# Spreading the choice of experts over 18 pairs of weight tiles, with GpSimd splitting the weights of the first 8

## The chip, the cores and the metric

The kernel runs on one core of one Trainium2 chip. The metric is device time in microseconds (us) of one execution; three timed runs of the kernel before gave 1732.83, 1733.56 and 1734.88 us, a median of 1733.56 us.

## The reference

Two transformer blocks over 256 tokens and 16 meta tokens, width 1024, all in float32. The change lies in the last layer, a mixture of 16384 small experts:

```python
def peer_layer(h, w_q, sub_keys, u_tab, v_tab):
    q = (hf @ w_q).reshape(T, PEER_HEADS, 2, PEER_DQ // 2)
    s = jnp.einsum('thpd,hpnd->thpn', q, sub_keys)
    sc, idx = lax.top_k(s, PEER_TOPK)                    # 16 of 128 keys, per head and half
    cand = (sc[:, :, 0, :, None] + sc[:, :, 1, None, :])  # 256 pairs
    top_sc, pos = lax.top_k(cand, PEER_TOPK)             # 16 of 256 pairs
    eidx = jnp.take_along_axis(cidx, pos, axis=-1)
    gate = jax.nn.softmax(top_sc)
    act = gelu(u_tab[eb] . hb)                           # per token, its 128 experts
    y = sum(gate * act * v_tab[eb])
```

There are 8 heads, 128 keys in each half, 256 tokens. What comes before (a first block with attention and two feed-forward parts, then a gated recurrence and a convolution) is not touched.

## The kernel before, in words

The kernel does not gather experts. It computes the activation of all 16384 experts for all 256 tokens, and multiplies by a gate that is zero for those not chosen. The table `peer_u` is 128 tiles of 128 x 1024 float32 (512 KB each). Matrix products are made exact enough by splitting every float32 operand into a high and a low part: `weights_by_part` (lines 89 to 101) loads a tile `wraw` by DMA, casts it to `whi` on ScalarE (ACT, L99), and subtracts, `wlo = wraw - whi` (L100), on VectorE (DVE) or, where the caller says so, on GpSimd (POOL). `mm3` (lines 116 to 119) then makes three matmuls of each 128 x 128 block on TensorE (PE): L117 and L118 with `whi`, L119 with `wlo`. A tile is 8 blocks, 24 matmuls. In the experts `wraw`, `whi` and `wlo` have three buffers each, so a tile's cast waits until PE is done with the tile three before it.

The loop over `m` goes over 64 pairs of tiles: `expert_acts(m, e)` makes the 48 matmuls of a pair, with `e` as the engine of the split, and a Gelu (ACT, L1351) takes the result to `acts`.

Beside it DVE chooses the experts. The generator `choosing` does this in steps, each ending at a `yield`: `keys_of(q)` for the last two heads (the others are done earlier, beside the query matmuls); `pairs(i)` for each half i of the tokens, which adds the two key scores to 256 candidates (L1234), casts indices (L1236), finds the best 16 for two heads in each step (`sixteen`, L1218 to L1222), and takes the found positions apart by two integer operations and a cast (L1241 to L1243); `members(i)`, which looks the indices up by a comparison (L1248), a product (L1250) and a sum (L1252). The loop over `m` advances the generator by two steps for each pair as long as `m < DIRECT`. From pair DIRECT on the softmax is made and `gates` builds the gate matrices, 64 of them, 1.5 for each pair.

The first `yield` in `keys_of` has no value, so `next(steps, 0)` gives None at the first step, and `alone` turns False in pair 0: the splits of all 64 pairs are on DVE in the program as built, and the trace shows none of `peer_u` on POOL.

A scheduler puts each engine's instructions into one fixed list; an engine runs its list in order, and waits at an instruction until its operands and buffers are there.

Of the kernel before, what the change touches and what calls it, by code (L numbers as in the profile page):

```python
# [46 lines left out]
def two_blocks(ctx: ExitStack, tc: tile.TileContext, A, out):  # L47
    nc = tc.nc
    act, vec, pool, pe = nc.scalar, nc.vector, nc.gpsimd, nc.tensor
# [34 lines left out]
    def bank(name):  # L84
        ids = banks[-1][name]
        ids.append(ids.pop(0))
        return ps.tile([128, 512], F32, name=name, tag=f"bank{ids[-1]}")
# [28 lines left out]
    def mm3(o, wh, wl, xh, xl, first, last):  # L116
        pe.matmul(o, lhsT=wh, rhs=xh, start=first, stop=False)  # L117
        pe.matmul(o, lhsT=wh, rhs=xl, start=False, stop=False)  # L118
        pe.matmul(o, lhsT=wl, rhs=xh, start=False, stop=last)  # L119
# [62 lines left out]
    with psum(mm=8):  # L182
        o = bank("mm")
# [925 lines left out]
    def experts(hx):  # L1109
        NEGL = -3.0e38  # L1110

        GATE = 2.0 ** 14
        DIRECT = 17
        PACE = 1.5
        es = ExitStack()
        early = ExitStack()
# [2 lines left out]
        def wt(ap, e=None, parts=1):  # L1119
            return weights(ap, e=e, parts=parts, four=False)  # L1120
# [8 lines left out]
        for i in range(2):  # L1129
            for e2 in range(2):  # L1130
                o = bank("sc")
# [10 lines left out]
        for n in range(6):  # L1142
            o = bank("mm")
            project(o[:, :S + 2], wt(A["peer_wq"][n], vec if n == 1 else pool), raw, t1=S + 2)
            rp.append(o)
            if n == 0:
                o = bank("sc")
# [76 lines left out]
        def keys_of(q):  # L1224
            for i in range(2):
                for e2 in range(2):
                    sixteen(best[i][:, q, e2], idx[i][:, q, e2], score(q, i)[:, e2])
            yield
# [3 lines left out]
        def pairs(i):  # L1232

            vec.tensor_tensor(out=cand[i], in0=best[i][:, :, 0][:, :, :, None].to_broadcast(wide),  # L1234
                              in1=best[i][:, :, 1][:, :, None, :].to_broadcast(wide), op=ALU.add)
            vec.tensor_copy(idf[i], idx[i])  # L1236
            for q in range(NH):
                sixteen(st[i][2][:, q], pos[i][:, q], cand[i][:, q].rearrange("p a b -> p (a b)"))
                if q % 2:
                    yield  # L1240
            vec.tensor_scalar(ab[i][:, 0], pos[i], 4, None, op0=ALU.logical_shift_right)  # L1241
            vec.tensor_scalar(ab[i][:, 1], pos[i], 15, None, op0=ALU.bitwise_and)
            vec.tensor_copy(abf[i], ab[i])  # L1243

        def members(i):

            for e2 in range(2):
                vec.tensor_tensor(out=cand[i], in0=abf[i][:, e2][:, :, :, None].to_broadcast(wide),  # L1248
                                  in1=iota[:, None, None, 0:TOPK].to_broadcast(wide), op=ALU.is_equal)
                vec.tensor_tensor(out=cand[i], in0=cand[i], in1=idf[i][:, :, e2][:, :, None, :].to_broadcast(wide), op=ALU.mult)  # L1250
                yield
                vec.tensor_reduce(out=st[i][e2], in_=cand[i], op=ALU.add, axis=AX.X)  # L1252
                yield

        def expert_acts(m, e):

            o = bank("mm")
            for e2 in range(2):
                hi, lo = wt(A["peer_u"][2 * m + e2], e)
                for k in range(KC):  # L1260
                    c = slice(k * 128, (k + 1) * 128)
                    mm3(o[:, e2 * S:(e2 + 1) * S], hi[:, c], lo[:, c], u3[k][0], u3[k][1], k == 0, k == KC - 1)
            return o.rearrange("p (a b) -> p a b", a=2)

        def softmaxes():

            for i in range(2):
                g = st[i][2]
                gs = pt.tile([128, NH], F32, name=f"gs{i}", bufs=1)
                vec.tensor_copy(gs, g[:, :, 0])  # L1270
                vec.tensor_sub(g, g, gs[:, :, None].to_broadcast([128, NH, TOPK]))
                tc.keep_in_program_order(act.activation(g, g, AF.Exp))
                vec.tensor_reduce(out=gs, in_=g, op=ALU.add, axis=AX.X)
                vec.reciprocal(gs, gs)
                vec.tensor_mul(g, g, gs[:, :, None].to_broadcast([128, NH, TOPK]))
                ts = slice(i * 128, (i + 1) * 128)
                o = bank("sc")
                for n in range(3):
                    tc.keep_in_program_order(pe.transpose(o[:, n * 128:(n + 1) * 128], st[i][n].rearrange("p a b -> p (a b)"), ident))
                vec.tensor_copy(tab[:, :, ts], o[:, :256].rearrange("p (a b) -> p a b", a=2))  # L1280
                vec.tensor_scalar(gtab[:, 1, ts], o[:, 256:384], GATE, None, op0=ALU.mult)

                half = pt.tile([128, 128], F16, name="half", bufs=1)
                vec.tensor_copy(half, gtab[:, 1, ts])
                vec.tensor_copy(gtab[:, 0, ts], half)
                vec.tensor_sub(gtab[:, 1, ts], gtab[:, 1, ts], gtab[:, 0, ts])
# [3 lines left out]
        def gates(t4, n):  # L1290

            o = bank("sc")
            ts = slice(4 * t4, 4 * t4 + 4)
            oij = pg.tile([128, 2, 4, 128], F16, name="oij")
            og = pg.tile([128, 2, 4, 128], F16, name="og")
            vec.tensor_tensor(out=oij, in0=iota[:, None, None, :].to_broadcast([128, 2, 4, 128]),  # L1296
                              in1=tab[:, :, ts][:, :, :, None].to_broadcast([128, 2, 4, 128]), op=ALU.is_equal)
            for part in range(2):
                if part and t4 % 2:
                    vec.tensor_mul(og[:, 1], oij[:, 1], gtab[:, 1, ts][:, :, None].to_broadcast([128, 4, 128]))  # L1300
                else:
                    for k in range(4):
                        act.activation(og[:, part, k], oij[:, 1, k], AF.Copy, scale=gtab[:, part, 4 * t4 + k:4 * t4 + k + 1])  # L1303
            for k in range(4):
                for part in range(2):
                    pe.matmul(o[:, k * 128:(k + 1) * 128], lhsT=og[:, part, k], rhs=oij[:, 0, k], start=part == 0, stop=part == 1)  # L1306
            gv = o.rearrange("p (n i) -> p i n", n=4)
            av = acts[:, :, ts]
            vec.tensor_mul(av[:, :n], av[:, :n], gv[:, :n])
            if n < KEYS:  # L1310
                act.copy(av[:, n:], gv[:, n:])
# [8 lines left out]
        def choosing():  # L1320

            for q in range(NH - 2, NH):
                yield from keys_of(q)
            for i in range(2):
                yield from pairs(i)
            yield None
            for i in range(2):
                yield from members(i)

        steps = choosing()  # L1330
        alone = True
        done = 0
        for m in range(KEYS // 2):
            if m < DIRECT:
                for n in range(2):
                    if next(steps, 0) is None and alone:
                        alone = False
            if m == DIRECT:
                for _ in steps:
                    pass  # L1340
                softmaxes()
                et.close()
                eg = ExitStack()
                pg = eg.enter_context(tc.tile_pool(name="exg", bufs=2))
            o = expert_acts(m, pool if alone else vec)
            a = acts[:, 2 * m:2 * m + 2]
            if done:
                t = qp.tile([128, 2, S], F32, name="pair")
                act.activation(t[:, :, :done], o[:, :, :done], AF.Gelu)  # L1349
            if done < S:  # L1350
                act.activation(a[:, :, done:], o[:, :, done:], AF.Gelu)  # L1351
            if done:
                vec.tensor_mul(a[:, :, :done], a[:, :, :done], t[:, :, :done])
            if m >= DIRECT:
                for _ in range(int((m - DIRECT + 1) * PACE) - int((m - DIRECT) * PACE)):
                    if done < S:
                        gates(done // 4, 2 * m + 2)
                        done += 4
# [62 lines left out]
    gated_mix()  # L1421
    stages.close()
    experts(hx)


# [133 lines left out]
```

## Time and profile before

| | us |
|---|---|
| three timed runs, median | 1733.56 |
| the profiled execution | 1733.11 |
| its span in the trace | 1731.1 |
| PE busy (97% of the span) | 1677.5 |
| DVE busy (75%) | 1306.5 |
| ACT busy (55%) | 947.4 |
| POOL busy (9%) | 155.0 |

The span is what the trace covers from the first to the last instruction; 2.0 us of the execution lie around it. Busy shares are means over stages with different limits: the page's row of 40 slices shows PE at 9 (90% or more) nearly everywhere, with one slice at 6 and one at 8 a little past the middle, where PE's clock row shows 7 and DVE stands at 9.

### The profile page before, as it was taken

To read this page: it belongs to the slowest core of one execution; us is meant where nothing else is said; L and a number is where in the kernel's file an instruction comes from. 1 tells how busy PE (TensorE), PEld (TensorE's weight loads), DVE (VectorE), ACT (ScalarE), POOL (GpSimd) and SP (SyncE) were. 2 spreads that over 40 slices of the span, in tenths; PEclk is the share of its full clock that TensorE was granted. 3 is DMA by queue.
4 is the path that set the end of the run, shared out by engine and by line. 5 is a ranking of instruction groups with operands and counts; after the bars stand their busy time and mean duration, and the time that the engine had idled before them with its cause. 6 is when DMAs were issued, how large, how long until landed. Compare 5 with 4: busy or idle time off the path is not lost.

```text
span 1731.1 us, 30677 instructions
## 1 busy us (share of the span) xinstructions
PE 1677.5 (97%) x11669; PEld 1547.6 (89%) x11669; DVE 1306.5 (75%) x2441; ACT 947.4 (55%) x1883; POOL 155.0 (9%) x119
## 2 busy tenths in 40 slices
PE   9999989999999999999998689999999999999997
PEld 8999977799999888889988689999999988888886
DVE  8887767589875777778889985788888666666665
ACT  6544455655544433326564235988888555555554
POOL 3001456230000000000053000000000000000000
PEclk9999999999999999999999799999999999999999
DMA  7877632068786333336554255455445575555563
GB/s 263 283 241 243 210 121 98 25 219 281 254 264 176 131 126 122 124 134 207 173 170 134 85 165 181 143 171 171 162 161 166 183 243 195 194 194 194 194 193 126
DMA packets 90483, 308.17 MB, mean 178 GB/s; under 512 B 11352, under 2 KB 13912, under 8 KB 90208
## 3 DMA queue, kind: packets, MB, share of 16 engines
q1 hardware_dynamic: 90336, 306.22, 54.0%
q8 instruction: 92, 1.51, 0.4%
q14 instruction: 55, 0.45, 0.1%
HBM read 304.08 MB, written 2.10 MB: 177 GB/s over the span
## 4 chain that ended last, share of the span: by engine, by line
PE 70%; DVE 6%; ACT 1%; issue 1%; DMA 0%; DVEq 0%; ACTq 0%
PE y L1375 20%; PE mm L119 12%; PE mm L117 12%; PE mm L118 11%; PE mm L811 11%; PE sc L1306 2%; DVE wlo L100 1%; PE lev L941 1%; DVE xl L742 1%; ACT whi L99 0%; DVE acts L1222 0%; PE mm L130 0%; PE lev L130 0%; DVE acts L1220 0%; DVE acts L1219 0%
## 5 line engine op out<-in xcount | busy, mean ns | idle before, releaser
L100 DVE TENSOR_TENSOR wlo<-wraw,whi 128x1024 fp32r<-128x1024 f32 (+2 forms) x444 | 534.6, 1209 | 196.1 <-ACT whi L99 193.8
L99 ACT CAST whi<-wraw 128x1024 fp32r<-128x1024 f32 (+2 forms) x476 | 484.8, 1022 | 360.1 <-PE mm L118 250.9
L119 PE MATMUL mm<-xh,wlo 128*128 128x256 f32 (+1 forms) x2044 | 586.5, 287 | 22.8 <-DVE wlo L100 22.8
L117 PE MATMUL mm<-xh,whi 128*128 128x256 f32 (+1 forms) x2044 | 592.6, 290 | 11.4 <-ACT whi L99 5.4
L118 PE MATMUL mm<-xl,whi 128*128 128x256 f32 (+1 forms) x2044 | 582.8, 285 | 2.7 <-DVE xl L168 1.5
L119 PEld LDWEIGHTS mm<-xh,wlo 128*128 128x128 f32 x2044 | 391.2, 191 | 24.5 <-DVE wlo L100 24.3
L117 PEld LDWEIGHTS mm<-xh,whi 128*128 128x128 f32 x2044 | 392.2, 192 | 16.5 <-ACT whi L99 6.5
L118 PEld LDWEIGHTS mm<-xl,whi 128*128 128x128 f32 x2044 | 392.4, 192 | 4.6 <-DVE xl L168 2.5
L811 PE MATMUL mm<-xw,wraw 128*128 128x256 f32 x848 | 197.5, 380 | 0.0
L811 PEld LDWEIGHTS mm<-xw,wraw 128*128 128x128 f32 x848 | 154.7, 190 | 19.2 <-issue 0.4
L1375 PE MATMUL y<-wlo,gah 128*128 128x512 f32 x512 | 158.0, 389 | 0.0
L1375 PE MATMUL y<-whi,gah 128*128 128x512 f32 x512 | 158.0, 389 | 0.0
L1375 PE MATMUL y<-whi,gal 128*128 128x512 f32 x512 | 157.8, 389 | 0.0
L1303 ACT ACTIVATE og<-oij,gtab 128x128 f16<-128x128 f16 x384 | 123.7, 394 | 20.3 <-DVE oij L1296 19.9
L175 ACT CAST gah<-acts 128x256 fp32r<-128x256 f32 x128 | 51.9, 407 | 149.8 <-PE y L1375 149.8
L850 DVE SCALAR_TENSOR_TENSOR cv<-glu,cols,cv 128x256 f32<-128x256 f32 x240 | 114.7, 478 | 3.0
L1375 PEld LDWEIGHTS y<-whi,gah 128*128 128x128 f32 x512 | 96.1, 188 | 20.3 <-ACT pair L1349 0.3
L1375 PEld LDWEIGHTS y<-wlo,gah 128*128 128x128 f32 x512 | 96.1, 188 | 20.2 <-DVE wlo L100 0.4
L1375 PEld LDWEIGHTS y<-whi,gal 128*128 128x128 f32 x512 | 96.1, 188 | 19.9
L100 POOL TENSOR_TENSOR wlo<-wraw,whi 128x1024 fp32r<-128x1024 f32 x32 | 77.2, 2417 | 362.3 <-ACT whi L99 361.9
L176 DVE TENSOR_TENSOR gal<-acts,gah 128x256 fp32r<-128x256 f32 x128 | 54.2, 424 | 59.8 <-PE y L1375 59.8
L1296 DVE TENSOR_TENSOR oij<-iota,tab 128x1024 f16<-128x1024 f32 x64 | 77.8, 1219 | 0.8 <-PE sc L1306 0.5
(898 smaller groups left out, 2289.0 us busy)
## 6 DMA issues: line engine op xcount, KB each, us to landing
wraw<-in_peer_u_dram SPq DMA_DIRECT2D x128, 512.0 KB, 3.3
wraw<-in_peer_v_dram SPq DMA_DIRECT2D x125, 512.0 KB, 4.3
wraw<-in_w_gu_dram SPq DMA_DIRECT2D x80, 512.0 KB, 4.5
wraw<-in_w_in_dram SPq DMA_DIRECT2D x80, 512.0 KB, 3.2
ada_w<-in_ada_w_dram SPq DMA_DIRECT2D x48, 512.0 KB, 4.8
wraw<-in_w_d_dram SPq DMA_DIRECT2D x32, 512.0 KB, 4.3
wraw<-in_w_out_dram SPq DMA_DIRECT2D x16, 512.0 KB, 3.3
wraw<-in_peer_wq_dram SPq DMA_DIRECT2D x16, 512.0 KB, 3.3
```

The lines of the kernel that those rows point to most:

```text
L99: act.copy(hi[:, c], raw[:, c])
L100: (e or vec).tensor_sub(lo[:, c], raw[:, c], hi[:, c])
L117: pe.matmul(o, lhsT=wh, rhs=xh, start=first, stop=False)
L118: pe.matmul(o, lhsT=wh, rhs=xl, start=False, stop=False)
L119: pe.matmul(o, lhsT=wl, rhs=xh, start=False, stop=last)
L175: act.copy(hi, x)
L176: vec.tensor_sub(lo, x, hi)
L811: pe.matmul(o, lhsT=w[:, k * 128:(k + 1) * 128], rhs=xw[k], start=k == 0, stop=k == KC - 1)
L850: tc.keep_in_program_order(vec.scalar_tensor_tensor(y, glu[:, j:j + S], cols[:, w0 + j:w0 + j + 1], y, op0=ALU.mult, op1=ALU.add))
L1296: vec.tensor_tensor(out=oij, in0=iota[:, None, None, :].to_broadcast([128, 2, 4, 128]), in1=tab[:, :, ts][:, :, :, None].to_broadcast([128 ...
L1303: act.activation(og[:, part, k], oij[:, 1, k], AF.Copy, scale=gtab[:, part, 4 * t4 + k:4 * t4 + k + 1])
L1375: pe.matmul(y[i][e2], lhsT=x[:, ts], rhs=v[:, e2 * 512:(e2 + 1) * 512], start=first and n == 0, stop=last and n == 2)
```

## The change

The choice is spread by a table `pace` over 18 pairs (DIRECT goes from 17 to 18): 1 step for each of the first 8 pairs, 2 in the fourth and eighth, then four pairs with one step and one with none, twice. The valueless step between `pairs` and `members` goes. POOL makes the splits of pairs 0 to 7, DVE from pair 8 on.

```diff
-        DIRECT = 17
+        DIRECT = 18
...
             for i in range(2):
                 yield from pairs(i)
-            yield None
             for i in range(2):
                 yield from members(i)
 
+
         steps = choosing()
-        alone = True
+        pace = (1, 1, 1, 2, 1, 1, 1, 2) + (1, 1, 1, 1, 0) * 2
         done = 0
         for m in range(KEYS // 2):
             if m < DIRECT:
-                for n in range(2):
-                    if next(steps, 0) is None and alone:
-                        alone = False
+                for n in range(pace[m]):
+                    next(steps)
...
-            o = expert_acts(m, pool if alone else vec)
+            o = expert_acts(m, pool if m < 8 else vec)
```

On DVE, where the search of the first half of the tokens (`eg_10254`) ends and that of the second (`eg_10257`) begins; a minus is the kernel before, a plus the changed one:

```order
 L1222 MAX_INDEX acts<-eg_10254,acts 128x8 x2
-L100 TENSOR_TENSOR wlo<-wraw,whi 128x1024 x2
+L1234 TENSOR_TENSOR acts<-acts 128x2048
 L1241 TENSOR_SCALAR acts<-acts 128x128
 L1242 TENSOR_SCALAR acts<-acts 128x128
-L1234 TENSOR_TENSOR acts<-acts 128x2048
+L1236 CAST acts<-acts 128x256
 L1243 CAST acts<-acts 128x256
-L1236 CAST acts<-acts 128x256
 L1218 MAX eg_10257<-acts 128x8 x2
```

The two splits are gone from here, and the same five small steps of the choice stand in another order.

On DVE, at the end of the second half's search, where the changed kernel has its first splits (those of pair 8) and the kernel before those of pair 4; of the kernel before:

```order
L1222 MAX_INDEX acts<-eg_10257,acts 128x8 x2
L100 TENSOR_TENSOR wlo<-wraw,whi 128x1024 x2
L1241 TENSOR_SCALAR acts<-acts 128x128
L1242 TENSOR_SCALAR acts<-acts 128x128
L1248 TENSOR_TENSOR acts<-acts,iota 128x2048
L1243 CAST acts<-acts 128x256
L1250 TENSOR_TENSOR acts<-acts 128x2048
L100 TENSOR_TENSOR wlo<-wraw,whi 128x1024 x2
L1252 TENSOR_REDUCE ei_10252<-acts 128x128
```

and of the changed one:

```order
L1222 MAX_INDEX acts<-eg_10257,acts 128x8 x2
L1248 TENSOR_TENSOR acts<-acts,iota 128x2048
L1241 TENSOR_SCALAR acts<-acts 128x128
L1242 TENSOR_SCALAR acts<-acts 128x128
L1250 TENSOR_TENSOR acts<-acts 128x2048
L1243 CAST acts<-acts 128x256
L100 TENSOR_TENSOR wlo<-wraw,whi 128x1024 x2
L1252 TENSOR_REDUCE ei_10252<-acts 128x128
L100 TENSOR_TENSOR wlo<-wraw,whi 128x1024
L1248 TENSOR_TENSOR acts<-acts,iota 128x2048
L100 TENSOR_TENSOR wlo<-wraw,whi 128x1024
L1250 TENSOR_TENSOR acts<-acts 128x2048
```

The first splits of pair 8 stand behind five steps of the choice; after that splits and steps take turns. POOL's list has 31 splits in a row at its end where it had 15: the 16 added are those of pairs 0 to 7.

## Rows read from the trace of the kernel before

**Rows 1.** The page's first line.
```profile
span 1731.1 us, 30677 instructions
```
**Rows 2.** Waits of PE, 925 to 1090 us: waiter, awaited, total, times, longest.
```profile
PE mm L119 <- DVE wlo L100: 22.1, 4, 11.9
PE mm L117 <- ACT whi L99: 5.4, 5, 1.4
```
**Rows 3.** Timeline of ACT, Gelus of pairs 8, 9 and 16: start us, us.
```profile
1026.82 0.59 ACT L1351 ACTIVATE acts<-mm 128x512 f32<-128x512 f32 x1
1032.50 0.59 ACT L1351 ACTIVATE acts<-mm 128x512 f32<-128x512 f32 x1
...
1072.26 0.59 ACT L1351 ACTIVATE acts<-mm 128x512 f32<-128x512 f32 x1
```
**Rows 4.** Timeline of PE in pair 1, second tile; idle before in brackets.
```profile
944.89 0.28 PE L117 MATMUL mm<-xh,whi 128*128 128x256 f32 x1
...
957.16 0.58 PE L119 MATMUL mm<-xh,wlo 128*128 128x256 f32 x1 [11.87 <-DVE wlo L100]
```
**Rows 5.** Windows, PE alone: stretch, us, busy (count), granted clock, DMA share, GB/s.
```profile
957.16:962.10 4.94, 4.94 (x22) 0.50 0.33 106
```
**Rows 6.** Timeline of DVE, 936 to 994 us, steps of the choice and splits.
```profile
936.79 0.48 DVE L1218 MAX8 acts<-acts 128x8 f32<-128x128 f32 x2
...
946.16 2.28 DVE L1234 TENSOR_TENSOR acts<-acts 128x2048 f32<-128x2048 f32 x1
...
966.62 0.22 DVE L1241 TENSOR_SCALAR acts<-acts 128x128 uint32<-128x128 uint32 x1
...
969.10 0.29 DVE L1243 CAST acts<-acts 128x256 f32<-128x256 uint32 x1
...
976.85 2.35 DVE L100 TENSOR_TENSOR wlo<-wraw,whi 128x1024 fp32r<-128x1024 f32 x2
...
986.46 2.35 DVE L100 TENSOR_TENSOR wlo<-wraw,whi 128x1024 fp32r<-128x1024 f32 x2
988.72 0.22 DVE L1241 TENSOR_SCALAR acts<-acts 128x128 uint32<-128x128 uint32 x1
...
993.60 2.36 DVE L100 TENSOR_TENSOR wlo<-wraw,whi 128x1024 fp32r<-128x1024 f32 x2
```
**Rows 7.** Timeline of ACT: the copy of the scores of head 6.
```profile
935.42 0.65 ACT L1214 COPY acts<-sc 128x256 f32<-128x256 f32 x2
```
**Rows 8.** Timelines of POOL and ACT, a split and a cast; landing of `wraw`, 871 to 936 us.
```profile
922.18 2.40 POOL L100 TENSOR_TENSOR wlo<-wraw,whi 128x1024 fp32r<-128x1024 f32 x1 [0.44 <-ACT whi L99]
...
941.89 1.05 ACT L99 CAST whi<-wraw 128x1024 fp32r<-128x1024 f32 x1 [1.79 <-PE mm L118]
...
DMA to landing us min/median/max: 3.1/3.3/4.2
```
**Rows 9.** Timelines of DVE and POOL, 871 to 876 us.
```profile
871.52 2.41 DVE L154 TENSOR_TENSOR ss_acc<-ss_acc,ss_sq 128x256 f32<-128x256 f32 x1 [0.79 <-ACT ss_sq L152]
...
875.77 0.41 DVE L154 TENSOR_TENSOR ss_acc<-ss_acc,ss_sq 128x256 f32<-128x256 f32 x1
...
871.25 2.40 POOL L100 TENSOR_TENSOR wlo<-wraw,whi 128x1024 fp32r<-128x1024 f32 x1 [317.29 <-ACT whi L99]
```
**Rows 10.** Timelines of DVE and POOL, 895 to 903 us.
```profile
896.42 4.65 DVE L742 SCALAR_TENSOR_TENSOR xl<-aff,ada,xh 128x256 fp32r<-128x256 f32 x2 [0.35 <-ACT xh L741]
...
895.66 7.65 POOL L100 TENSOR_TENSOR wlo<-wraw,whi 128x1024 fp32r<-128x1024 f32 x3 [2.37 <-ACT whi L99]
```
**Rows 11.** Line 549, 280 to 340 us (ns min/median/max); then DVE and POOL at 294 us.
```profile
L549 DVE TENSOR_SCALAR P<-P,sums x32: 279/349/2499, 285.6 to 336.5; 128x144 f32<-128x144 f32 x16, 128x272 f32<-128x272 f32 x16
...
294.21 2.70 DVE L549 TENSOR_SCALAR P<-P,sums 128x144 f32<-128x144 f32 x2
...
294.39 2.36 POOL L100 TENSOR_TENSOR wlo<-wraw,whi 128x1024 fp32r<-128x1024 f32 x1 [8.04 <-ACT whi L99]
```
**Rows 12.** Instructions on `acts`: a search over keys, ns min/median/max, first and last start.
```profile
L1218 DVE MAX8 acts<-acts x32: 268/274/294, 901.8 to 944.0; 128x8 f32<-128x128 f32 x32
```

## The prediction

> **What bounds the kernel now.** I read the page's head first, then PE's waits, then the timelines of the stretch where PE waits. The span is 1731.1 us [rows 1], and PE fills nearly all of it, so the question is where it does not. Between 925 and 1090 us PE waits 22.1 us in four pieces for a low part that DVE had not made, and 5.4 us in five pieces for a high part [rows 2]. That stretch is the choice of experts, where DVE's splits stand in its list behind searches.
>
> What the stretch loses comes out of the Gelus, one after each pair. Undisturbed pairs follow each other by 1032.50 - 1026.82 = 5.68 us [rows 3], so a tile takes 2.84 us and a matmul 0.118 us. Pair 1's second tile begins at 944.89 [rows 4], so pair 1 began 24 matmuls earlier, at 942.06. Pair 16 ends at 1072.26 [rows 3]. Sixteen pairs took 130.2 us where 16 x 5.68 = 90.9 would do: 39.3 us are lost. Of these 27.5 are the waits of [rows 2]. Most of the other 11.8 are the clock: after the wait of 11.87 us [rows 4] the granted clock is 0.50, the lower of PE's two levels (1.2 of 2.4 GHz), and 22 matmuls take 4.94 us instead of 2.6 [rows 5], a loss of 2.3. 39.3 us is thus the most that the change can give back.
>
> **The change, part by part.**
>
> *Pairs 0 to 7, the splits.* 16 splits leave DVE. On POOL one takes 2.40 us, one per tile of 2.84 us [rows 8], so POOL is busy 85% of the time and can follow. Latency: the buffers allow a split to start two tiles (5.68 us) before it is wanted, and the cast (1.05 [rows 8]) plus POOL's 2.40 with their hand-overs are 3.7 of it, so a split may be about 2.2 us late before PE notices. A buffer of `wraw` goes round in landing (3.3, at most 4.2 us) [rows 8], cast and split, some 7 to 8 us, where three tiles give 8.52. I take no loss of PE in pairs 0 to 7; the bound from the other side is 0.2 us per tile if every transfer were slow, 3 us in all. Pair 8 then begins at 942.06 + 7 x 5.68 = 981.8, and its first low part is wanted at 982.06.
>
> *DVE without splits, and nothing in its way.* The choice from the first search of head 6, at 936.79, to the end of `pairs(1)`, at 986.46 [rows 6], took 49.67 us, with five splits inside, one alone and twice two as at 976.85. Two take 2.26 us from start to start (986.46 to 988.72), so the choice alone is 49.67 - 5 x 1.13 = 44.0 us. It can start when the scores of head 6 are copied, about 935.9 [rows 7], so it would end at 980.0. Then come the comparison, the product and three small steps, 993.60 - 988.72 = 4.88 us [rows 6], and only then the first split of pair 8, 1.15 us with its hand-over: 986.0. PE would wait 4.0 us.
>
> *DVE against POOL.* Rows speak against that. An addition of DVE (L154) with both operands in SBUF takes 0.41 us alone, and 2.41 us when it comes 0.27 us after POOL's split: it ends as POOL ends [rows 9]. Of two subtractions (L742) that stand together, both wait, one split of POOL each, 4.65 us, while POOL's three splits take 7.65 [rows 10] instead of 7.2: the two engines take turns, one instruction each, and POOL loses little. A TENSOR_SCALAR within SBUF (L549), 0.28 or 0.35 us else, took 2.50 [rows 11] when POOL began at the same moment. The searches do not wait: 32 of them lie between 268 and 294 ns, whether POOL splits (to 928 us) or not [rows 12].
>
> So of the choice's steps in pairs 0 to 7 seven are exposed: the two additions L1234, and L1236, L1241, L1242, L1236, L1243. Additions are the kind of [rows 9]. The shifts are the kind of [rows 11]. For the casts no row shows a meeting. Bounds: nothing, or a POOL split each, 2.40. I take the upper, as the cast's 0.29 us for 256 elements against the shift's 0.22 for 128 [rows 6] is 0.5 ns an element, the rate of L549 (0.07 us for 128 more), which did wait.
>
> The Trainium skill's page "SBUF — State Buffer", section "Who interferes with whom", has the rule: cast and tensor_scalar can take both of DVE's port pairs, one of them shared with GpSimd, and then whichever began first blocks the other for a whole instruction; a tensor_tensor with both inputs in SBUF blocks too. By that rule the three casts cost 3 x 2.5 us, by the rows without it possibly nothing; the sum would be 1713 or 1705. The trace agrees with it for tensor_tensor (2.41 for 0.41 us) and tensor_scalar (2.50 for 0.28), and is silent on casts.
>
> Now in time. POOL's splits start every 2.84 us and leave gaps of 0.44; the one behind the cast of 941.89 [rows 8] starts some 1.1 us later and runs until 945.4. Searches of heads 6 and 7 (9.37 us, from 936.79 to 946.16 [rows 6]) end at 945.25; the addition waits 0.2 and holds POOL to 947.75. POOL's split that waited goes first, so the cast ends at 950.4. Searches of the first half, 14.7 us (as those from 969.5, behind the casts at 969.1, to 986.46 less two splits [rows 6]), end at 965.1. The second addition meets a split that ends at 965.3, and, 2.28 us long [rows 6], runs to 967.6. Now L1241, L1242, L1236 and L1243 stand together, POOL is a split behind, and each lets one split by: 4 x 2.55 = 10.2, to 977.8. By then POOL has made its sixteenth split. Searches, 14.7, end at 992.5. Against 980.0 DVE is 12.5 us late; the additions' waits could each be 0 to 2.4 longer, the last cast's 2.4 shorter.
>
> POOL is itself held at most 2.3 us, twice, by an addition: the same as its slack.
>
> *Pair 8 and after.* The first split of pair 8 ends at 992.5 + 4.9 + 1.2 = 998.6. PE waits from 982.06: 16.5 us, then 2.3 us more at the lower clock, as in [rows 5]. Behind it, a pair costs DVE two splits (2.3) and on average 3.3 us of `members` (comparison, product and sum in every two pairs, 2.2 each if the sum is taken as long as the others), 5.6 of PE's 5.68, and two of the ten pairs have no step. Going through the list, each low part is there 0.1 to 1.5 us before PE wants it. I add nothing.
>
> *DIRECT 18.* Softmax and gates come one pair later; 64 gates at 1.5 per pair end in pair 60 of 64 instead of 59, and the page's slices show PE at 9 there. Nothing.
>
> **Sum.** Lost before 39.3; lost after 16.5 + 2.3 = 18.8; gain 20.5. From the profiled execution's 1733.11 us: 1712.6. The median of the runs is 0.45 above it, so 1713.
>
> **Rivals.**
> - *The small steps pass together.* After one split of POOL all four (and the cast after the first addition) run at once, or the casts do not wait. DVE is then 5 us late instead of 12.5, PE waits 9 us: 1705. For it: each is only 0.2 us long, and POOL may hand over slowly. Against: [rows 10].
> - *No meeting matters.* PE waits 4.0 us and loses 2.2 to the clock: gain 33, 1700. Against: [rows 9 to 11].
> - *POOL doesn't follow.* Splits held by DVE's additions, or slow transfers, let PE wait inside pairs 0 to 7, with waits of 1 to 3 us that also bring the lower clock: 5 to 8 us on top of the forecast, though DVE then gains time against PE; 1716 to 1720. For it: 85% of POOL is used; against: the slack of 2.2 us.
> - *Slower.* The searches wait as well, so that DVE and POOL run in turns throughout: 14 splits of 2.40 lie beside the searches, 33.6 us; the first split of pair 8 ends at 1019.6, PE waits 37.6 + 2.3: 39.9 lost against 39.3, 1734. It decides from 33 us of waiting on DVE, that is if about every search of the 256 candidates met a split. Against: [rows 12], for searches over 128; those over 256 never met POOL.
> - *The splits stay where they are.* Then pairs 0 to 7 are as before; the lists show 16 more on POOL, so this is excluded.
>
> **How the numbers follow.** The forecast has 0.56, from 1709 to 1717 by the bounds of the single waits; the small steps together 0.24; no meeting 0.08; POOL too slow 0.08; slower 0.04, half of it within the 0.2% (3.5 us) that a measurement tells from no change. The range takes in the no-meeting case and most of the slow-POOL one, 1699 to 1719. Faster: 0.96, same 0.02, slower 0.02.
>
> **What would show it.** Right: 16 splits of 2.4 us on POOL from 928 to 978 us; PE without waits to 982; L1236, L1241, L1242 and L1243 at some 2.4 us each; one wait of 14 to 19 us for the low part of pair 8, clock 0.50 for 5 us behind it, none later. Wrong: waits of PE before 980; small steps at 0.2 to 0.3 us; a search of 256 candidates above 0.5 us; or low parts late in pairs 9 to 17.

## The result and the profile after

The changed kernel takes 1712.83 us (median of four runs, 1711.79 to 1714.31) against 1733.19 us for the kernel before on the same chip: a ratio of 0.9884 with a 95% interval of 0.9869 to 0.9900. 1713 us were forecast.

The profiled execution took 1711.79 us, 21.3 less than that of before. The stretch in question accounts for nearly all of it. The copy of head 6's scores starts at 934.52 instead of 935.42 [rows 7], 0.9 us that come from earlier stages, which the change does not touch. The Gelu of pair 16 starts at 1051.01 instead of 1072.26 [rows 3], 21.25 earlier; 20.35 of that arise between the two. What follows pair 16 is as long as before (658.9 against 658.8 us to the end of the span).

PE's waits between 925 and 1090 us, where [rows 2] had nine pieces and 27.5 us:

```profile
PE mm L119 <- DVE wlo L100: 16.6, 2, 15.9
```

The timeline of PE shows the long one, at the first L119 of pair 8, and the windows the clock behind it (stretch, us, busy and count, granted clock, DMA share, GB/s):

```profile
980.79 0.28 PE L118 MATMUL mm<-xl,whi 128*128 128x256 f32 x1
997.01 0.58 PE L119 MATMUL mm<-xh,wlo 128*128 128x256 f32 x1 [15.94 <-DVE wlo L100]
```

```profile
997.01:1002.00 4.99, 4.99 (x25) 0.55 0.65 212
1002.00:1008.00 6.00, 6.00 (x53) 1.00 0.53 176
```

One wait of 15.94 us stands where nine stood. (The second piece, 0.69 us at 1077.65, lies behind pair 16; the kernel before has the same 0.69 at 1093.21.) Behind the long one 25 matmuls take 4.99 us at a mean granted clock of 0.55, so most of the time at the lower of PE's two levels, the 0.50 of [rows 5]; at the pace of the next row (53 in 6.00) they would take 2.8, so the clock costs some 2.2 us. The Gelus put both into one number. These are those of pairs 7, 8 and 16, on ACT:

```profile
981.74 0.59 ACT L1350 ACTIVATE acts<-mm 128x512 f32<-128x512 f32 x1
1005.57 0.59 ACT L1350 ACTIVATE acts<-mm 128x512 f32<-128x512 f32 x1
...
1051.01 0.59 ACT L1350 ACTIVATE acts<-mm 128x512 f32<-128x512 f32 x1
```

Pair 8 comes 23.83 us after pair 7, 18.15 more than the 5.68 of an undisturbed pair. From pair 8 to 16 it is 45.44 = 8 x 5.68: nothing is lost there.

Why DVE was late is in its own timeline, the steps of the choice other than searches; POOL's splits of the same time stand below:

```profile
944.29 2.42 DVE L1234 TENSOR_TENSOR acts<-acts 128x2048 f32<-128x2048 f32 x1
946.64 2.49 DVE L1236 CAST acts<-acts 128x256 f32<-128x256 uint32 x1
...
963.75 2.99 DVE L1234 TENSOR_TENSOR acts<-acts 128x2048 f32<-128x2048 f32 x1
966.66 2.42 DVE L1241 TENSOR_SCALAR acts<-acts 128x128 uint32<-128x128 uint32 x1
969.00 2.44 DVE L1242 TENSOR_SCALAR acts<-acts 128x128 uint32<-128x128 uint32 x1
971.36 2.50 DVE L1236 CAST acts<-acts 128x256 f32<-128x256 uint32 x1
973.78 2.48 DVE L1243 CAST acts<-acts 128x256 f32<-128x256 uint32 x1
...
993.07 0.21 DVE L1241 TENSOR_SCALAR acts<-acts 128x128 uint32<-128x128 uint32 x1
...
995.75 2.34 DVE L100 TENSOR_TENSOR wlo<-wraw,whi 128x1024 fp32r<-128x1024 f32 x2
```

```profile
945.01 8.76 POOL L100 TENSOR_TENSOR wlo<-wraw,whi 128x1024 fp32r<-128x1024 f32 x3 [0.45 <-ACT whi L99]
955.08 9.51 POOL L100 TENSOR_TENSOR wlo<-wraw,whi 128x1024 fp32r<-128x1024 f32 x4 [1.31 <-ACT whi L99]
964.88 11.24 POOL L100 TENSOR_TENSOR wlo<-wraw,whi 128x1024 fp32r<-128x1024 f32 x4 [0.30 <-ACT whi L99]
```

The same instructions that took 0.22 and 0.29 us in [rows 6] take 2.4 to 2.5 us while POOL splits, five times in all. None of these rows has an idle time in brackets: the waiting counts as the instruction's own time, so a list of waits does not show it. At 993.07, with POOL done since 976.12, L1241 is back at 0.21. The last four (966.66 to 976.26) lie beside POOL's last four splits (964.88 to 976.12), which take 11.24 us in place of 4 x 2.40 = 9.6, as the first of them is held by the addition. Two more traces of this choice, of the runs at pair 17 and of the changed kernel again (both below), have the same five at 2.42 to 2.51 us.

The searches over 256 candidates, of which the trace of before had none beside POOL, are unaffected. The first row is the line by shape of the changed kernel (us busy, mean ns, idle before) for 950 to 963 us, the second the same line of the kernel before (ns min/median/max, first and last start):

```profile
L1221 DVE MAX8 eg<-acts 128x8 f32<-128x256 f32 x8 | 3.0, 411 | 0.0
```

```profile
L1221 DVE MAX8 eg<-acts x16: 410/419/427, 950.8 to 985.3; 128x8 f32<-128x256 f32 x16
```

### The profile page after: what moved, and what is told of

It reads as the page before. It is cut to its first block, busy times and chain, and to the rows that moved or that the text cites. A ratio compares the mean times of both kernels' runs of the same rounds, so it can differ in the third digit from the quotient of the medians.

```text
span 1709.9 us, 30681 instructions
## 1 busy us (share of the span) xinstructions
PE 1666.5 (97%) x11669; PEld 1537.7 (90%) x11669; DVE 1300.1 (76%) x2424; ACT 946.6 (55%) x1883; POOL 196.3 (11%) x135
## 4 chain that ended last, share of the span: by engine, by line
PE 70%; DVE 6%; ACT 2%; issue 1%; DMA 0%; DVEq 0%; ACTq 0%
PE y L1374 20%; PE mm L117 11%; PE mm L119 11%; PE mm L118 11%; PE mm L811 11%; PE sc L1306 2%; PE lev L941 1%; DVE xl L742 1%; ACT whi L99 1%; DVE acts L1222 0%; DVE acts L1220 0%; DVE acts L1219 0%; DVE wlo L100 0%; PE mm L130 0%; PE lev L130 0%
## 5 line engine op out<-in xcount | busy, mean ns | idle before, releaser
L100 DVE TENSOR_TENSOR wlo<-wraw,whi 128x1024 fp32r<-128x1024 f32 (+2 forms) x428 | 515.7, 1209 | 176.2 <-ACT whi L99 173.3
L119 PE MATMUL mm<-xh,wlo 128*128 128x256 f32 (+1 forms) x2044 | 581.9, 285 | 17.1 <-DVE wlo L100 17.0
L119 PEld LDWEIGHTS mm<-xh,wlo 128*128 128x128 f32 x2044 | 386.6, 189 | 18.0 <-DVE wlo L100 17.9
L117 PEld LDWEIGHTS mm<-xh,whi 128*128 128x128 f32 x2044 | 387.5, 190 | 10.6 <-DVE fk L337 4.8
L118 PEld LDWEIGHTS mm<-xl,whi 128*128 128x128 f32 x2044 | 388.1, 190 | 5.3 <-DVE xl L168 3.0
L100 POOL TENSOR_TENSOR wlo<-wraw,whi 128x1024 fp32r<-128x1024 f32 x48 | 118.7, 2483 | 369.8 <-ACT whi L99 369.4
```

The lines of the kernel that those rows point to most:

```text
L100: (e or vec).tensor_sub(lo[:, c], raw[:, c], hi[:, c])
```

## The experiments

The theory: in pairs 0 to 7, DVE's additions, casts and integer operations within SBUF cannot run while POOL reads SBUF, and wait for its split; this puts DVE some 12 us behind, and PE meets it at pair 8. Rivals: the pace alone is the gain, or POOL's splits alone; or the long wait at pair 8 has another cause. All ratios are to the kernel before, in the same batch.

**The two parts one by one.** First the pace without POOL:

```diff
-            o = expert_acts(m, pool if m < 8 else vec)
+            o = expert_acts(m, vec)
```

> The changed kernel with the splits of pairs 0 to 7 back on DVE: the pace alone. If the gain needs both parts, or comes mainly from GpSimd, the time goes back towards 1733. My account: DVE's work in pairs 0 to 7 is 44.0 (choice) + 16 x 1.13 (splits) = 62 us against 45.4 us of PE, so PE loses about 17 us in several short waits plus some 4 us of the lower clock, and from pair 8 on DVE's 5.6 us per pair fit PE's 5.68. Lost 21 against 18.8 in the changed kernel: 1715 us, between 1709 and 1720. GpSimd's part then buys almost nothing, since what DVE saves on splits it gives back in waits for the port.

Measured: 1714.74 us, ratio 0.9901 (0.9885 to 0.9918). PE's waits:

```profile
PE mm L119 <- DVE wlo L100: 9.0, 8, 2.2
PE mm L117 <- ACT whi L99: 5.2, 5, 1.6
```

14.2 us in 13 pieces, none over 2.2 us. Without POOL's splits the small steps, which the changed kernel has at 2.4 to 2.5 us, are short:

```profile
970.77 0.22 DVE L1241 TENSOR_SCALAR acts<-acts 128x128 uint32<-128x128 uint32 x1
...
973.24 0.29 DVE L1243 CAST acts<-acts 128x256 f32<-128x256 uint32 x1
```

The pace alone brings nearly the whole gain. POOL's splits add 1.9 us by the medians and 2.9 by the ratios; as the two intervals overlap, a gain from them alone is not shown.

Then POOL without the pace, in the kernel before:

```diff
-            o = expert_acts(m, pool if alone else vec)
+            o = expert_acts(m, pool if m < 8 else vec)
```

> The kernel before with one edit: GpSimd splits for pairs 0 to 7; two steps for each pair and DIRECT 17 as before. My account: DVE's list has nearly the whole choice ahead of the first split of pair 8: 44.0 us + 12.5 us of waits beside GpSimd + about 24 us of lookups, so PE waits some 35 us there, plus 2.3 at the lower clock, 37 of the 39.3 lost before: 1730.5 us, between 1726 and 1734. Rival (GpSimd's splits are the gain, the pace matters little): 1713.

Measured: 1729.32 us, ratio 0.9984 (0.9974 to 0.9993), a gain of 0.16%. PE loses its time in one piece, at pair 8:

```profile
PE mm L119 <- DVE wlo L100: 32.8, 2, 32.1
```

The two parts are no sum. POOL takes away the splits between the searches, but leaves everything that DVE has not done by pair 8 in one wait, here 32.07 us; with the pace that wait is 15.94.

**Taking the small steps out of POOL's time.** In `pairs` and `members`:

```diff
 def pairs(i):
     vec.tensor_tensor(out=cand[i], ...)
-    vec.tensor_copy(idf[i], idx[i])
...
-    vec.tensor_scalar(ab[i][:, 0], pos[i], 4, None, op0=ALU.logical_shift_right)
-    vec.tensor_scalar(ab[i][:, 1], pos[i], 15, None, op0=ALU.bitwise_and)
-    vec.tensor_copy(abf[i], ab[i])
 def members(i):
+    vec.tensor_copy(idf[i], idx[i])
+    vec.tensor_scalar(ab[i][:, 0], pos[i], 4, None, op0=ALU.logical_shift_right)
+    vec.tensor_scalar(ab[i][:, 1], pos[i], 15, None, op0=ALU.bitwise_and)
+    vec.tensor_copy(abf[i], ab[i])
```

> The changed kernel with the casts and integer operations (L1236, L1241 to L1243) moved from pairs() to members(), that is behind GpSimd's last split. Five waits of 2.4 us on DVE should go (the two additions stay beside GpSimd): the small steps take 0.2 to 0.3 us again, the wait for the low part of pair 8 falls from 15.9 to 4 us, and the time to 1701.5 us (1699 to 1705). Rival (the wait at pair 8 has another cause, or GpSimd's splits hold DVE whatever it does): the time stays at 1712.8.

Measured: 1699.41 us, ratio 0.9812 (0.9796 to 0.9828). DVE, where the two additions now stand together, and PE at pair 8:

```profile
943.90 6.82 DVE L1234 TENSOR_TENSOR acts<-acts 128x2048 f32<-128x2048 f32 x2
...
980.03 0.28 DVE L1243 CAST acts<-acts 128x256 f32<-128x256 uint32 x1
980.22 0.22 DVE L1244 TENSOR_SCALAR acts<-acts 128x128 uint32<-128x128 uint32 x1
...
983.24 1.22 DVE L100 TENSOR_TENSOR wlo<-wraw,whi 128x1024 fp32r<-128x1024 f32 x1
984.37 2.28 DVE L1250 TENSOR_TENSOR acts<-acts 128x2048 f32<-128x2048 f32 x1
```

```profile
953.02 0.39 PE L119 MATMUL mm<-xh,wlo 128*128 128x256 f32 x1 [0.74 <-POOL wlo L100]
...
984.51 0.58 PE L119 MATMUL mm<-xh,wlo 128*128 128x256 f32 x1 [2.83 <-DVE wlo L100]
```

The small steps cost 0.2 to 0.3 us again, and the wait at pair 8 shrinks by 13.1 us, from 15.94 to 2.83. Not all of that is their doing. DVE's first split of pair 8 starts 12.5 us earlier (983.24 for 995.75): 11.0 us are the five waits that are gone, from start to start in the rows. 2.2 us come from the list, which now has the product L1250 behind that split and not ahead of it; 0.8 are an earlier start of the stretch and two small steps that also moved behind; and the two additions, now together, take 1.5 us more. The rest is on PE's side, which asks 0.6 us later: the additions hold POOL, so PE waits 0.74 us for a split of POOL at 953.02, the loss in pairs 0 to 7 that the changed kernel does not have. 11.0 of the 15.94 us are thus the waits of the five steps, and the rival of another cause falls.

**What kind of instruction waits.** The casts as sums over one element, at the same places:

```diff
-            vec.tensor_copy(idf[i], idx[i])
+            vec.tensor_reduce(out=idf[i], in_=idx[i][:, :, :, :, None], op=ALU.add, axis=AX.X)
...
-            vec.tensor_copy(abf[i], ab[i])
+            vec.tensor_reduce(out=abf[i], in_=ab[i][:, :, :, :, None], op=ALU.add, axis=AX.X)
```

> The changed kernel with the casts L1236 and L1243 written as sums over an axis of one element (TENSOR_REDUCE, the same values, at the same places in DVE's list). If DVE waits because a cast within SBUF takes the port that GpSimd uses, and a sum does not, the three sums beside GpSimd take 0.3 to 0.4 us instead of 2.5: 6.3 us less, 1706.5 us (1704 to 1709, as the later steps meet GpSimd's splits at other moments). Rival (any short DVE instruction behind a waiting one lets a split by): the sums take 2.5 us too, 1712.8.

Measured: 1701.08 us, ratio 0.9830 (0.9809 to 0.9851): a larger gain than expected, outside the range of 1704 to 1709. DVE and POOL at the second addition, and PE at pair 8:

```profile
961.53 2.26 DVE L1234 TENSOR_TENSOR acts<-acts 128x2048 f32<-128x2048 f32 x1
963.72 0.21 DVE L1241 TENSOR_SCALAR acts<-acts 128x128 uint32<-128x128 uint32 x1
963.86 0.21 DVE L1242 TENSOR_SCALAR acts<-acts 128x128 uint32<-128x128 uint32 x1
964.00 0.40 DVE L1236 TENSOR_REDUCE acts<-acts 128x256 f32<-128x256 uint32 x1
```

```profile
961.91 4.43 POOL L100 TENSOR_TENSOR wlo<-wraw,whi 128x1024 fp32r<-128x1024 f32 x1 [0.43 <-ACT whi L99]
```

```profile
985.60 0.58 PE L119 MATMUL mm<-xh,wlo 128*128 128x256 f32 x1 [4.66 <-DVE wlo L100]
```

The sums take 0.40 us beside POOL, as expected, where casts took 2.5 at the same places: it is the kind of instruction that waits. The three of them make 6.3 of the 11.3 us by which PE's wait shrinks, the two integer operations 4.4 and the additions 0.7. These last two were not foreseen. The addition now began in the gap before POOL's split and did not wait; the split was held instead (4.43 for 2.40), and L1241 and L1242 ran at 0.21 behind the addition before POOL came in. In the changed kernel, where the addition itself had waited, POOL came in after each single instruction. One of the four runs of this kernel took 1707.05 us, the other three 1699.77 to 1701.15; no trace shows where its addition fell.

**Is it the moment that decides?** Three more sums move that addition by 1 us, and do nothing else:

```diff
             vec.tensor_reduce(out=idf[i], in_=idx[i][:, :, :, :, None], op=ALU.add, axis=AX.X)
+            if i == 0:
+                for d in spare:
+                    vec.tensor_reduce(out=d, in_=idx[i][:, :, :, :, None], op=ALU.add, axis=AX.X)
```

> The kernel with the casts as sums, with three more such sums (into spare memory, not used) right behind the first: they wait for nothing, 0.33 us each, and only move the second half's addition by 1.0 us, out of the gap between two of GpSimd's splits (where it fell with the casts as sums, and where the two integer operations behind it then were not held) into the middle of one. If that moment decides, the addition waits about 2 us and L1241 and L1242 take 2.4 us each again: 1.0 + 2 + 4.4 = 7.4 us more than with the sums alone, 1708.5 us (1706 to 1710). Rival (the integer operations ran free because the steps around them are sums): 1.0 us more for the sums and up to 2.4 for the addition, 1702 to 1704.5.

Measured: 1708.07 us, ratio 0.9867 (0.9850 to 0.9883).

```profile
962.37 3.94 DVE L1235 TENSOR_TENSOR acts<-acts 128x2048 f32<-128x2048 f32 x1
966.24 2.43 DVE L1245 TENSOR_SCALAR acts<-acts 128x128 uint32<-128x128 uint32 x1
968.59 2.45 DVE L1246 TENSOR_SCALAR acts<-acts 128x128 uint32<-128x128 uint32 x1
970.96 0.41 DVE L1237 TENSOR_REDUCE acts<-acts 128x256 f32<-128x256 uint32 x1
```

```profile
961.77 2.40 POOL L100 TENSOR_TENSOR wlo<-wraw,whi 128x1024 fp32r<-128x1024 f32 x1 [0.38 <-ACT whi L99]
```

```profile
992.56 0.58 PE L119 MATMUL mm<-xh,wlo 128*128 128x256 f32 x1 [11.77 <-DVE wlo L100]
```

The same instructions, 1 us later: the addition meets a split that began at 961.77, and both integer operations wait again. Some 1 us of work at the wrong moment costs 7.0 us by the medians (6.4 by the ratios), and in the traces PE's wait grows by 7.1 us, from 4.66 to 11.77. That a DVE that has waited lets POOL in after each instruction, and one that has not goes on, fits these runs; what decides it inside the chip they do not show.

**Do the waits add up?** Two more casts behind the first L1236 of the changed kernel:

```diff
             vec.tensor_copy(idf[i], idx[i])
+            if i == 0:
+                for d in spare:
+                    vec.tensor_copy(d, idx[i])
```

> The changed kernel with two more casts of the first half's indices (into spare memory, not used) right behind L1236 of the first half. If a cast beside GpSimd lets a split by, each takes 2.4 us, where the cast alone is 0.2 to 0.3. What they cost in the end is less: DVE comes to the second half's small steps 4.8 us later, when GpSimd has one or two splits fewer left, so one or two of the four waits there go: 0 to 2.5 us more than the changed kernel in all. Rival (every wait adds up): 4.8 us more. Rival (casts wait for nothing of GpSimd's): 0.4 us more, and 0.2 us each in the trace.

Measured: 1712.37 us, ratio 0.9886 (0.9870 to 0.9903), beside 0.9889 for the changed kernel in the same batch (below).

```profile
948.99 4.89 DVE L1240 CAST acts<-acts 128x256 f32<-128x256 uint32 x2
...
974.48 2.45 DVE L1246 TENSOR_SCALAR acts<-acts 128x128 uint32<-128x128 uint32 x1
976.85 0.28 DVE L1237 CAST acts<-acts 128x256 f32<-128x256 uint32 x1
977.06 0.28 DVE L1247 CAST acts<-acts 128x256 f32<-128x256 uint32 x1
```

```profile
970.51 6.34 POOL L100 TENSOR_TENSOR wlo<-wraw,whi 128x1024 fp32r<-128x1024 f32 x2 [0.44 <-ACT whi L99]
```

```profile
998.08 0.58 PE L119 MATMUL mm<-xh,wlo 128*128 128x256 f32 x1 [17.07 <-DVE wlo L100]
```

Each added cast takes 2.4 us. The two at the end no longer wait, since POOL has nothing left to split by then (its last split ends at 976.85): PE's wait grows from 15.94 to 17.07 only, and the time does not move by what a run can tell. Here DVE pays one split of POOL for each exposed step, as long as POOL has splits left.

**One pair earlier.** `DIRECT = 17` with the rest as changed, and the changed kernel again beside it:

> The changed kernel with softmax and gates from pair 17 instead of 18 (the last pair of the pace has no step, so nothing else moves). If PE is full behind the choice, one pair earlier is worth nothing: the same time as the changed kernel within 0.2%. Rival (the gates are crowded at the end, so that starting later costs): 1 to 3 us less.

> The changed kernel itself, beside the others of this batch: 0.988 of the kernel before, about 1712 us.

Measured: 1712.54 us, ratio 0.9885 (0.9869 to 0.9902), against 1713.24 us, 0.9889 (0.9873 to 0.9906). The intervals lie on each other: where the gates begin is worth nothing that these runs show.

**A better version.** On top of the small steps behind POOL's time, the two splits of pair 8 before the lookups:

```diff
                 hi, lo = wt(A["peer_u"][2 * m + e2], e)
+                if m == 8 and e2:
+                    vec.tensor_scalar(nil, lo[:, 0:1].bitcast(F32), 0.0, None, op0=ALU.mult)
...
-            vec.tensor_copy(abf[i], ab[i])
+            vec.tensor_scalar(abf[i], ab[i], nil, None, op0=ALU.add)
...
-        pace = (1, 1, 1, 2, 1, 1, 1, 2) + (1, 1, 1, 1, 0) * 2
+        pace = (1, 1, 1, 2, 1, 1, 1, 2) + (0, 1, 1, 1, 1, 0, 1, 1, 1, 1)
```

> The variant with the small steps moved behind GpSimd's splits, and the lookups held back, by a data dependence on a 128x1 zero made from the low part of pair 8, until DVE has made the two splits of pair 8; pace 0 in pairs 8 and 13. DVE should reach the first split of pair 8 some 2 us earlier than in that variant, so PE waits 1 us instead of 2.8 there, and the lower clock behind it may stay away: 1696.5 us (1694.5 to 1698.5). Rival (the wait of 2.8 us is made up later anyway, or comes back at pairs 9 to 12 since DVE's lookups move later): 1699.4.

Measured: 1696.76 us, ratio 0.9795 (0.9779 to 0.9811). At pair 8 PE waits 1.15 us, and the window behind it has the upper clock:

```profile
984.06 0.39 PE L119 MATMUL mm<-xh,wlo 128*128 128x256 f32 x1 [1.15 <-DVE wlo L100]
```

```profile
984.06:990.00 5.94, 5.94 (x50) 1.00 0.56 179
```

This is the fastest of the kernels run, 16 us below the changed one. Against the version with the 2.83 us wait (1699.41) it gains 2.6 us by the medians; the two were timed in different batches and their intervals overlap, though no run of the one is as fast as any of the other (1696.04 to 1697.46, and 1699.03 to 1700.24). 1.7 us are the wait itself; behind the longer wait the clock was 0.73 over 5.5 us.

## Why the prediction was right

- *The loss of 39.3 us as the most that can come back.* 20.35 us of it came back between head 6's scores and pair 16, 20.5 were forecast. No run went beyond the 39.3: the fastest kernel is 35.3 us below the kernel before in its batch (1732.04 to 1696.76).
- *No loss in pairs 0 to 7.* Right: PE has no wait before 981. One cast came late (953.95, after 3.34 us of waiting for its transfer), behind splits that DVE had held, and the slack of 2.2 us covered it.
- *The seven exposed steps.* All seven waited: five small ones at 2.42 to 2.50 us, the additions took 2.42 and 2.99 for 2.28, so waited 0.1 and 0.7. The upper bound taken for the casts was the right one. The Trainium skill's page "SBUF — State Buffer", section "Who interferes with whom", says that casts can contend with GpSimd and that on this chip a tensor_reduce never does; the traces agree, with 2.49 us for a cast of 0.29 and 0.40 us for a sum beside a split.
- *The wait at pair 8.* 15.94 for 16.5, as the stretch began 0.9 us earlier and the moments fell nearly as worked out: the first split of pair 8 started at 995.75, where 997.4 was forecast, or 996.5 with the 0.9 off. Clock: some 2.2 for 2.3 us.
- *Pair 8 and after, and DIRECT 18.* Nothing lost from pair 8 to 16; DIRECT is worth nothing by experiment.
- *The rival of the searches that wait* is out: 411 ns for 256 candidates beside POOL, 410 to 427 without.
- *What the prediction did not see.* It credited the gain to the splits leaving DVE. The pace alone reaches 1714.74 us: all but 2 to 3 us of what POOL's help saves is given back in the waits that it causes. And the turns of DVE and POOL, taken as strict from [rows 10], are not: where an addition has not waited itself, the next steps pass as well, as in the version with sums at 1701.08. That the forecast took the other case came out right by luck of the moment: in the changed kernel the second addition was due during a split, at 963.75, 0.8 us before that split ended (964.59) and POOL's gap of 0.3 us began.

## What to carry to other kernels

Work given to GpSimd to relieve VectorE can be paid for by VectorE's own short instructions: before moving a split, list which of VectorE's steps beside it are casts or integer tensor_scalars (2.4 us each here, for 0.2 to 0.3) or tensor_tensors within SBUF (2.41 for 0.41 in [rows 9]), and put these where GpSimd rests; searches and sums may stay. And where two engines share a stretch, ask what each part of an edit brings alone: here the pace was the gain, and with GpSimd's help the kernel came 15 us below the pace alone (1714.74 to 1699.41) only after five small instructions had been moved, or 13.7 (1701.08) with the casts as sums at their old places. What these two edits do without GpSimd's help was not run; as each step takes 0.2 to 0.4 us in either form where POOL does not split, little is expected of them.

## What was not expected of the hardware

A cast of 0.29 us can cost 2.5 us, and 1 us of harmless work ahead of an addition cost 7.0 us in all (1701.08 to 1708.07): it moved the addition out of a gap of 0.4 us between two splits (961.48 to 961.91) into a split, and two further instructions had to wait with it.
